# Product 2 of two groups as one block product, rows scaled by halves, loads one at a time

## Chip, cores and metric

One core of a Trainium2 chip. The metric is the device time of one execution in microseconds (us), the median of several runs.

## What is computed

```python
def reference(a, b, gamma, eps):          # a, b: 2048 x 2048 f32, gamma: 2048
    x = np.matmul(a, b)
    rms = np.sqrt(np.mean(x ** 2, axis=-1, keepdims=True) + eps)
    return (gamma * x / rms).astype(np.float32)
```

A matrix product, then each row is divided by its root mean square and multiplied by gamma.

## The kernel before

**Tiling.** `a` is cut into 16 row blocks of 128, `b` stays in SBUF in bf16 (`raw[j][kp]`: half j of N, 1024 columns, and 256 rows of K). Two row blocks, 2g and 2g+1, form a *group* g. Blocks 0 to 3 are the head (plain products, and one group that is partly transformed); groups 2 to 7 are worked by `first_segment`, `segment` and `last_group`, lines 550 to 729, and only these are changed.

**Seven products for eight.** For a group and a half of N, the 256 x 2048 by 2048 x 1024 product is split in two by two by two (rows by block, K into even and odd tiles of 128, columns into chunks of 512), and made with Winograd's seven products: `product(g, j, m, bank)` for m = 1 to 7, each eight matmuls of 128x128 by 128x512 (`KP` = 8) into one PSUM bank. Product 1 is A11 B11 and product 2 is A12 B21. The right-hand sums lie in `sums[j]` and, for one of them, in place in `raw`; the left-hand sums `s_sum` are made for each group by `a_sums(g, which)` on VectorE from the transposed row blocks `at(2g)` and `at(2g+1)`. Sum 2 is the left operand of product 6, sum 3 of product 7, sum 4 of product 3, sum 1 (in place in the odd block) of product 5.

**Half groups and segments.** `halves` lists (g, j); n is the index, so n = 0 is group 2 left, n = 4 group 4 left, n = 10 and 11 group 7. `do(n, m)` issues product m of half group n; `take(n, what)` moves a result out of PSUM into an `x` tile in SBUF. Partial results pass from bank to bank: after product 1, ScalarE copies bank B1 to B2 (line 528); product 6 adds into B2; ScalarE copies B2 to B3 (530); product 5 adds into B3; VectorE's `take 22` makes the bottom right chunk of B3 and of product 7 (which ScalarE copied, 532); product 4 adds into B2 and `take 21` makes the bottom left; product 3 adds into B3, and `take 12` (540) is the top right; product 2 adds into B1, and `take 11` (538) is the top left. So product 3 has to wait for take 22, which reads the bank that it adds to.

`segment(n)` issues, in this order, product 6 of n, product 3 of n-1, product 2 of n, product 1 of n+1, products 7, 5 and 4 of n. Around them it weaves the work on the rows to come and on those that are done. The order of each engine's work is the order of the program (`manual_schedule`): an instruction that waits holds up all behind it on its engine.

**Rows to come.** A row block is loaded to `a32` (two buffers, on POOL's queue). In the left segment of group g, blocks 2g+2 and 2g+3 are readied: `row_norm` (two squares and a root on ScalarE), `prepare` = `row_factor` (four small VectorE operations), `row_apply` (scale to fp16, 2048 wide, line 240), `transpose_dma` (on SP's queue, line 199). In the right segment `a_sums(g + 1, ...)` makes the sums from them. `load_after(src, mb)` has POOL copy one column of `src` (line 140), so that the load of block mb is issued only when `src` is there; in a left segment the load of 2g+4 follows the transposed block 2g+2, in a right one that of 2g+5 follows the transposed block 2g+3.

**Rows that are done.** `square_half` and `square_right` square x on ScalarE (line 267), the latter with the root; `finish` (line 306) multiplies both halves by 1/rms and gamma on VectorE and issues the outputs on SP. Blocks 2g-1 and 2g-2 are finished in the left segment of group g. x tiles are eight slots, shared out by `slot_of` (line 248).

**The end.** `last_group` has its own order for group 7 (lines 630 to 729): product 2 of its right half, then `square_of`, root and inverse for block 14, product 7, then product 4 of the left half and sixteen matmuls of 256 columns for block 15, whose sums are added to the banks on VectorE before (line 699).

Of the kernel before, what the change touches and what calls it, by code (L numbers as in the profile page):

```python
# [17 lines left out]
def kernel(  # L18
# [13 lines left out]
    nc = tc.nc  # L32
# [11 lines left out]
    NG = MB // 2  # L44
    G0 = HB // 2
    PAIR = G0 - 1

    ctx.enter_context(tc.manual_schedule())
    consts = ctx.enter_context(tc.tile_pool(name="consts", bufs=1))
# [32 lines left out]
    def a16_slot(mb):  # L82
        if mb == HB + 1:
            return a16_first
        if mb == HB:
            return x_slot[2 * HB - 1].bitcast(FP16)
        return head_flat.bitcast(FP16)[:, (2 + mb % 2) * K:(3 + mb % 2) * K]

    s_sum = {s: consts.tile([P, KP, P], FP16, name=f"s_{s}") for s in (2, 3, 4)}

    def at(mb):
        return (at_even, at_odd)[(mb // 2) % 2][:, mb % 2]
# [105 lines left out]
    def transpose_dma(mb):  # L198
        nc.sync.dma_start_transpose(at(mb), a16[mb])
# [17 lines left out]
    def row_norm(mb):  # L217
        n2 = stat_pool.tile([P, 2], FP32, name="n2")
        for h in range(2):
            junk = sq_pool.tile([P, 2 * CH], BF16, name="sq")  # L220
            nc.scalar.activation(out=junk, in_=a32[mb][:, h * HALF:(h + 1) * HALF],  # L221
                                 func=ACTF.Square, scale=2.0 ** -8, accum_out=n2[:, h:h + 1])
        norm[mb] = stat_pool.tile([P, 1], FP32, name="norm")
        nc.scalar.activation(out=norm[mb], in_=n2[:, 0:1], func=ACTF.Sqrt, bias=n2[:, 1:2],  # L224
                             scale=1.0)
# [12 lines left out]
    def row_apply(mb):  # L238
        a16[mb] = a16_slot(mb)
        nc.vector.tensor_scalar_mul(out=a16[mb], in0=a32.pop(mb), scalar1=factor.pop(mb))  # L240

    def prepare(mb):
        row_factor(mb)
        row_apply(mb)
        transpose_dma(mb)

    x_half = {}
    slot_of = {(r, h): r + HB * h for r in range(HB) for h in range(2)}

    for n, slots in enumerate(((0, 4, 1, 5), (2, 6, 3, 7), (4, 5, 0, 1), (6, 7, 2, 3),  # L250
                               (5, 1, 4, 0), (7, 3, 6, 2))):
        for m, slot in enumerate(slots):
            slot_of[HB + 2 * n + m % 2, m // 2] = slot

# [15 lines left out]
    def square_half(mb, h):  # L270
        square_of(mb, x_tile(mb, h))
# [73 lines left out]
    def product_matmul(g, j, m, bank, kp, start):  # L345
        lhsT = {1: lambda: quarter(g, 0, 0), 2: lambda: quarter(g, 0, 1),
                3: lambda: sum_of(g, 4), 4: lambda: quarter(g, 1, 1), 5: lambda: sum_of(g, 1),
                6: lambda: sum_of(g, 2), 7: lambda: sum_of(g, 3)}[m]()
        rhs = {1: lambda: b_quarter(j, kp, 0, 0), 2: lambda: b_quarter(j, kp, 1, 0),
               3: lambda: b_quarter(j, kp, 1, 1), 4: lambda: sums[j][:, 2, kp, :],  # L350
               5: lambda: b_quarter(j, kp, 0, 1), 6: lambda: sums[j][:, 0, kp, :],
               7: lambda: sums[j][:, 1, kp, :]}[m]()
        nc.tensor.matmul(bank, lhsT[:, kp, :], rhs, start=(start and kp == 0),  # L353
                         stop=(kp == KP - 1), skip_group_check=not start)

    def product(g, j, m, bank, start=True):
        for kp in range(KP):
            product_matmul(g, j, m, bank, kp, start)

# [157 lines left out]
    def do(n, m, copies=True):  # L519

        if n >= len(halves) or n < 0:
            return
        g, j = halves[n]
        b1, b2, b3 = B1[n % 2], B2[n % 2], B3[n % 2]
        product(g, j, m, {1: b1, 2: b1, 3: b3, 4: b2, 5: b3, 6: b2, 7: B7}[m],
                start=m in (1, 7))
        if m == 1:
            nc.scalar.copy(out=b2, in_=b1)  # L528
        elif m == 6:
            nc.scalar.copy(out=b3, in_=b2)  # L530
        elif m == 7 and copies:
            nc.scalar.copy(out=chunks(n)[2], in_=B7)  # L532

    def take(n, what, engine="A"):

        x11, x12, x21, x22 = chunks(n)
        if what == 11:
            copy_on(engine)(out=x11, in_=B1[n % 2])
        elif what == 12:
            copy_on(engine)(out=x12, in_=B3[n % 2])  # L540
        elif what == 22:
            add(x22, B3[n % 2], x21)
        else:
            add(x21, B2[n % 2], x21)

    def load_after(src, mb):
        wait_for(src)
        load_block(mb)

    def first_segment():  # L550
        n, g, j = 0, G0, 0
        nxt = 2 * g + 2
        do(n, 1)
        do(n, 7, False)
        finish(0, (1,))
        pair_ends()
        do(n, 2)
        row_norm(nxt)
        a_sums(g, (4,))
        finish(0, (0,))  # L560
        do(n, 6)
        do(n + 1, 1)
        prepare(nxt)
        do(n, 5)
        nc.scalar.copy(out=chunks(n)[2], in_=B7)
        take(n, 22)
        row_norm(nxt + 1)
        take(n, 11)
        finish(1)
        do(n, 4)  # L570
        prepare(nxt + 1)
        load_after(at(nxt + 1)[:, KT - 1, 0:1], nxt + 2)
        take(n, 21)
        square_half(2 * g + 1, j)

    def segment(n):
        g, j = halves[n]
        ra, rb, nxt = 2 * g, 2 * g + 1, 2 * g + 2
        more = g + 1 < NG
        do(n, 6)  # L580
        if j == 0:
            finish(ra - 1)
            if more:
                row_norm(nxt)
        elif g == G0:
            square_right(r2)
        do(n - 1, 3)
        take(n - 1, 12)
        if j == 0:
            square_right(ra - 2)  # L590
            if more:
                prepare(nxt)
            a_sums(g, (4,))
            finish(ra - 2)
        else:
            square_half(ra, 0)
            if g == G0:
                square_right(r3)
                finish(r2, (1, 0))
        do(n, 2)  # L600
        take(n, 11)
        do(n + 1, 1)
        if j == 0 and more:
            row_norm(nxt + 1)
        if j == 1 and g + 2 < NG:
            load_after(at(nxt + 1)[:, KT - 1, 0:1], nxt + 3)
        if j == 1 and more:
            a_sums(g + 1, (1, 2))
        do(n, 7)
        if j == 1 and more:  # L610
            a_sums(g + 1, (3,))
        do(n, 5)
        take(n, 22)
        if j == 1:
            take_pre(rb)
            take_pre(ra)
        do(n, 4)
        take(n, 21)
        if j == 0:
            square_half(rb, 0)  # L620
            if more:
                prepare(nxt + 1)
            if g + 2 < NG:
                load_after(at(nxt)[:, KT - 1, 0:1], nxt + 2)
        else:
            square_right(rb)
            if g == G0:
                finish(r3, (1, 0))

    def last_group():  # L630
        n = len(halves) - 2
# [11 lines left out]
        def by_r(x, r):  # L643
            nc.scalar.activation(out=x, in_=x, func=ACTF.Copy, scale=r)  # L644

        b2, b3 = [B2[(n + j) % 2] for j in range(2)], [B3[(n + j) % 2] for j in range(2)]
        do(n, 6)
        finish(rb - 2)
        do(n - 1, 3)
        take(n - 1, 12)  # L650
        square_right(ra - 2)
        a_sums(g, (4,))
        do(n, 2)
        take(n, 11)
        do(n + 1, 1)
        do(n, 5)
        nc.scalar.copy(out=x22[0], in_=b3[0])
        finish(ra - 2)
        do(n + 1, 6)
        do(n, 7)  # L660
        add(x22[0], x21[0], x22[0])
        add(b2[0], b2[0], x21[0])
        square_of(rb, x22[0])
        do(n + 1, 5)
        nc.scalar.copy(out=x22[1], in_=b3[1])
        wide = a_pool.tile([P, K], FP32, name="a32")
# [5 lines left out]
        take(n, 12)  # L672
        square_half(ra, 0)
        add(xa, xa, gam_left, ALU.mult)
        do(n + 1, 3)
        take(n + 1, 12)
        square_of(ra, x12[1])
        add(x12[1], x12[1], gam[3], ALU.mult)
        pre_a = stat_pool.tile([P, 1], FP32, name="pre")
        nc.vector.tensor_scalar(out=pre_a, in0=msq[ra][:, 0:1], scalar1=msq[ra][:, 1:2],  # L680
                                scalar2=msq[ra][:, 2:3], op0=ALU.add, op1=ALU.add)
        do(n + 1, 2)
        take(n + 1, 11)
        square_of(ra, x11[1])
        rms_a = root(msq[ra][:, 3:4], pre_a)
        r_a = inverse(rms_a)
        other = B1[0]
        product(g, 1, 7, other)
        nc.scalar.copy(out=x21[1], in_=other)
        halves2 = [slice(0, CH // 2), slice(CH // 2, CH)]  # L690
# [3 lines left out]
        nc.sync.dma_start(out=rows(ra, 0, CH), in_=left)  # L694
        nc.gpsimd.tensor_scalar_mul(out=mid, in0=mid, scalar1=r_a)  # L695
        nc.sync.dma_start(out=rows(ra, CH, HALF), in_=mid)
        nc.vector.tensor_scalar_mul(out=x12[1], in0=x12[1], scalar1=r_a)
        for bank, col in zip(half, halves2):
            add(bank, b2[1][:, col], x21[1][:, col])
        add(x22[1], x21[1], x22[1])  # L700
        scaled_gamma(x11[1], x11[1], r_a, gam[2])
        nc.sync.dma_start(out=rows(ra, HALF, N), in_=x_tile(ra, 1))
        do(n, 4)
        square_of(rb, b2[0])
# [64 lines left out]
```

## Time and profile before

| | |
|---|---|
| median of 3 runs | 223.53 us (223.38 to 223.86) |
| the profiled execution | 222.88 us |
| its span in the trace | 221.1 us |
| mean granted TensorE clock | 0.996 of full speed |
| segments 0 to 9 on TensorE | from 67.3 to 189.65 us |
| last group on TensorE | 189.65 to 214.0 us |
| scaling of a row block to fp16, line 240 | 1.28 us |
| add of a PSUM chunk to an x tile, line 98 | 0.69 us |
| one row block, load to landing | 4.9 to 10.7 us |
| one row block, transpose to landing | 4.2 to 7.2 us |

The span is the time between the first and the last instruction of the trace; the execution's own time has 1.8 us around it. In the trace, PE is TensorE's matmuls, PEld its weight loads, DVE is VectorE, ACT ScalarE, SP and POOL the two queues that issue DMAs (SPq, POOLq). A row of a timeline has the start, the duration, the engine, the line of the program, the operation with its output and inputs, the count, and in brackets the idle time before it with what ended that. A matmul is shown with 0.38 us for its whole way through the array, while the next one starts 0.216 us after it.

### The profile page before, as it was taken

The page shows a single profiled execution, that of the slowest core. Times are in us where ns is not written, and L with a number is a line of the kernel's source. Part 1 is how long each engine was busy: PE and PEld are TensorE (multiplying, and loading weights), DVE is VectorE, ACT ScalarE, POOL GpSimd, SP SyncE. Part 2 cuts the span into 40 slices and gives each one's busy share as a digit, 9 for nine tenths or more (in the row PEclk, how much of TensorE's full clock was granted, in tenths as well). Part 3 has the DMA queues.
Part 4 walks back from the last instruction along what each step waited for, and adds up shares of the span by engine and source line. Part 5 has one row for each costly group of instructions (what it writes and reads, how often), then busy time and mean ns, then how long its engine had stood idle before and what let it go on. Part 6 is the DMA issues. An engine that isn't in the chain of part 4 may idle for free.

```text
span 221.1 us, 2897 instructions
## 1 busy us (share of the span) xinstructions
PE 208.3 (94%) x1012; PEld 97.4 (44%) x1032; DVE 144.4 (65%) x281; ACT 115.7 (52%) x229; POOL 37.7 (17%) x74
## 2 busy tenths in 40 slices
PE   7699999999999999999998999999999999999970
PEld 3344544444454444444443444444444444444440
DVE  2128779999999984988506981688246953583381
ACT  2110002900698558679624966296627964364781
POOL 8544443443000001200101010201010000000030
PEclk9999999999999999999999999999999999999998
DMA  7999999999957486899884499458965874063044
GB/s 147 174 201 205 203 206 210 211 208 237 414 159 329 193 245 135 252 399 342 279 250 193 190 285 284 174 204 224 278 98 213 187 251 86 1 246 138 0 187 193
DMA packets 36719, 46.59 MB, mean 211 GB/s; under 512 B 22240, under 2 KB 26336, under 8 KB 35424
## 3 DMA queue, kind: packets, MB, share of 16 engines
q0 software_dynamic: 10608, 23.86, 43.9%
q1 hardware_dynamic: 25824, 22.29, 33.1%
q10 hardware_dynamic: 272, 0.26, 0.3%
q8 instruction: 8, 0.13, 0.2%
q14 instruction: 7, 0.06, 0.1%
HBM read 34.60 MB, written 16.78 MB: 232 GB/s over the span
## 4 chain that ended last, share of the span: by engine, by line
PE 65%; issue 11%; DMA 10%; ACT 7%; DVE 3%; POOL 1%; ACTq 0%; POOLq 0%; DVEq 0%
PE acc L353 46%; PE acc L366 15%; ACT sq L221 4%; DMA a<-in_a_dram 4%; DMA at_even<-head_at 3%; DMA early<-in_a_dram 3%; PE tbank L392 2%; PE tbank L176 2%; ACT sq L267 1%; DVE a_first L240 1%; POOL b L112 0%; ACT norm L224 0%; ACT sq L717 0%; POOL pace L140 0%; ACT a L644 0%
## 5 line engine op out<-in xcount | busy, mean ns | idle before, releaser
L267 ACT ACTIVATE sq<-x 128x1024 bf16<-128x1024 f32 (+1 forms) x33 | 33.2, 1005 | 30.5 <-DVE x L98 26.6
L353 PEld LDWEIGHTS <-s 128*128 128x128 f16 (+1 forms) x312 | 30.4, 98 | 38.4 <-DVE s L330 1.5
L366 PE MATMUL acc<-b,head_at 128*128 128x512 bf16 x171 | 42.3, 379 | 1.7 <-DMA b<-in_b_dram 1.6
L353 PE MATMUL acc<-b,head_at 128*128 128x512 bf16 x164 | 40.8, 379 | 0.3
L306 DVE SCALAR_TENSOR_TENSOR x<-x,r,gamma_sb 128x1024 f32<-128x1024 f32 x28 | 34.8, 1282 | 0.5
L353 PE MATMUL acc<-b,at_even 128*128 128x512 bf16 x142 | 33.3, 379 | 0.1
L353 PEld LDWEIGHTS <-head_at 128*128 128x128 f16 (+1 forms) x216 | 21.0, 98 | 24.8
L353 PEld LDWEIGHTS <-at_even 128*128 128x128 f16 x192 | 18.8, 98 | 22.6
L353 PE MATMUL acc<-early,s 128*128 128x512 bf16 x108 | 27.1, 379 | 0.2
L221 ACT ACTIVATE sq<-a 128x1024 bf16<-128x1024 f32 x24 | 25.3, 1056 | 1.6 <-DMA a<-in_a_dram 1.2
L366 PEld LDWEIGHTS <-head_at 128*128 128x128 bf16 x176 | 16.9, 98 | 20.8 <-issue 1.7
L353 PE MATMUL acc<-b,s 128*128 128x512 bf16 x103 | 24.3, 379 | 0.3 <-DVE x L98 0.2
L353 PE MATMUL acc<-t_left,s 128*128 128x512 bf16 x95 | 22.5, 379 | 1.0 <-DVE s L330 1.0
L112 POOL DMA_DIRECT2D b<-in_b_dram x32 | 17.2, 540 | 20.8 <-DMA b<-in_b_dram 14.2
L98 DVE TENSOR_TENSOR x<-acc,x 128x512 f32<-128x512 f32 x23 | 15.9, 690 | 6.0 <-ACT x L532 3.3
L402 ACT COPY x<-acc 128x512 f32<-128x512 f32 x7 | 4.1, 580 | 25.5 <-PE acc L366 25.5
L240 DVE TENSOR_SCALAR head_at<-a,s 128x2048 f16<-128x2048 f32 x10 | 12.8, 1278 | 0.0
L330 DVE TENSOR_TENSOR at_even<-at_even 128x1024 f16<-128x1024 f16 x3 | 2.1, 692 | 14.0 <-DMA at_even<-head_at 14.0
L181 DVE COPY head_at<-tbank 128x1024 bf16<-128x1024 bf16 x7 | 4.8, 692 | 9.2 <-PE tbank L176 9.2
L528 ACT COPY acc<-acc 128x512 f32<-128x512 f32 x12 | 6.9, 578 | 6.7 <-PE acc L353 6.7
L695 POOL TENSOR_SCALAR x<-x,r 128x512 f32<-128x512 f32 x1 | 1.9, 1852 | 46.5 <-DVE r L288 46.5
L288 DVE RECIPROCAL r<-rms 128x1 f32<-128x1 f32 x16 | 2.6, 160 | 10.8 <-ACT rms L283 10.7
(103 smaller groups left out, 207.4 us busy)
## 6 DMA issues: line engine op xcount, KB each, us to landing
out_dram<-x SPq DMA_DIRECT2D x29, 512.0 KB, 3.2
a<-in_a_dram POOLq DMA_DIRECT2D x10, 1024.0 KB, 6.0
b<-in_b_dram POOLq DMA_DIRECT2D x32, 256.0 KB, 10.1
a<-in_a_dram POOLq DMA_DIRECT2D x4, 512.0 KB, 9.8
early<-in_a_dram POOLq DMA_DIRECT2D x7, 256.0 KB, 10.2
gamma_sb<-in_gamma_dram POOLq DMA_DIRECT2D x2, 512.0 KB, 9.9
out_dram<-x SPq DMA_DIRECT2D x3, 256.0 KB, 2.5
out_dram<-a SPq DMA_DIRECT2D x1, 768.0 KB, 3.3
```

What stands on the lines that cost most here:

```text
L98: nc.vector.tensor_tensor(out=out, in0=in0, in1=in1, op=op)
L112: nc.gpsimd.dma_start(out=raw[j][kp][:, t, :], in_=b[lo:lo + P, j * HALF:(j + 1) * HALF])
L176: nc.tensor.matmul(view[:, t, r, :], ah(kp)[:, r, t * P:(t + 1) * P], identity, is_transpose=True, start=(t == 0 and r == 0), stop=(t == 1 ...
L181: nc.vector.tensor_copy(out=head_at[:, 2 * kp:2 * kp + 2, :, :], in_=view)
L221: nc.scalar.activation(out=junk, in_=a32[mb][:, h * HALF:(h + 1) * HALF], func=ACTF.Square, scale=2.0 ** -8, accum_out=n2[:, h:h + 1])
L240: nc.vector.tensor_scalar_mul(out=a16[mb], in0=a32.pop(mb), scalar1=factor.pop(mb))
L267: nc.scalar.activation(out=sq[:, 0:src.shape[-1]], in_=src, func=ACTF.Square, scale=inv_sqrt_n, accum_out=msq[mb][:, c:c + 1])
L306: nc.vector.scalar_tensor_tensor(out=x, in0=x, scalar=inverse_of[mb], in1=gamma_sb[:, h * HALF:(h + 1) * HALF], op0=ALU.mult, op1=ALU.mult)
L353: nc.tensor.matmul(bank, lhsT[:, kp, :], rhs, start=(start and kp == 0), stop=(kp == KP - 1), skip_group_check=not start)
L366: nc.tensor.matmul(bank, head_at[:, kt, r, :], head_rhs(c, kt), start=(kt == 0), stop=(kt == KT - 1))
L392: nc.tensor.matmul(tbank, head_at[:, 2 * kp + t, g[0], :], head_rhs(g[1], 2 * kp + t), start=(t == 0), stop=(t == 1))
L528: nc.scalar.copy(out=b2, in_=b1)
```

## The change

Groups 4 and 5 form a pair, and so do 6 and 7. Product 2 is left out of the halves of these groups. In its place one block product is made for the pair: the A12 of two groups (two row blocks) by the B21 of both halves of N, with K cut in two, is again a two by two by two product, and is made with seven steps of four matmuls (`KQ` = 4) for eight. `step(g, m, bank)` issues a step. Its right-hand sums (`b_two`, 16 adds of 512) are made once, in segments 3 to 5; its left-hand sums (`a_two_sums`, four adds of 512) for each pair, in the right segment of its first group, between that segment's a_sums. The steps are woven into `block_segment`, which takes the place of segment 6, and into `last_group`. The bank of the transposes, `tbank`, and the two B1 banks become X2, W2 and Y2.

From product 1 of group 4 on, product 1 goes straight to bank B2, and ScalarE copies it to the top left x chunk, to which the block's result is added later by VectorE. So the squares and the finish of a pair's first row block come later: `finish(8)` in segment 7, `finish(12)` in the last group after product 7.

From row block 10 on, `prepare` scales a row by halves of 1024 and transposes each half with a DMA of its own; the second half lands in the row's own f32 buffer. The loads of blocks 2g+4 and 2g+5 are now both issued in the right segment of group g, the first after block 2g+3 is transposed, the second after the first has landed.

```diff
+    G2 = G0 + 2
+    KQ = KP // 2
...
+    t_two = {2: a16_first.bitcast(BF16), 3: head_flat[:, 2 * K:3 * K], 4: head_flat[:, 3 * K:4 * K]}
+    t_two = {s: t.rearrange("p (k n) -> p k n", k=KQ) for s, t in t_two.items()}
+    y_two = x_slot[5].bitcast(FP16).rearrange("p (s k m) -> p s k m", s=4, k=KQ)
+    a16_half = consts.tile([P, HALF], FP16, name="a16_half")
...
     def prepare(mb):
         row_factor(mb)
-        row_apply(mb)
-        transpose_dma(mb)
+        if mb < 2 * (G2 + 1):
+            row_apply(mb)
+            transpose_dma(mb)
+            return
+        src, f = a32.pop(mb), factor.pop(mb)
+        for h, dst in enumerate((a16_half, src.bitcast(FP16)[:, 0:HALF])):
+            nc.vector.tensor_scalar_mul(out=dst, in0=src[:, h * HALF:(h + 1) * HALF], scalar1=f)
+            nc.sync.dma_start_transpose(at(mb)[:, h * KP:(h + 1) * KP, :], dst)
...
+    def b_two(s):
+        for k in range(KQ):
+            z11, z12, z21, z22 = (z_two(h, j, k) for h in range(2) for j in range(2))
+            out, x, y = {1: (z12, z12, z11), 2: (t_two[2][:, k, :], z22, z12),
+                         3: (t_two[3][:, k, :], z22, z12),
+                         4: (t_two[4][:, k, :], z21, t_two[2][:, k, :])}[s]
+            add(out, x, y, ALU.subtract)
...
+    def a_two_sums(g):
+        a11, a12, a21, a22 = (a_two(g, r, h) for r in range(2) for h in range(2))
+        y1, y2, y3, y4 = (y_two[:, n] for n in range(4))
+        add(y3, a11, a21, ALU.subtract)
+        add(y1, a21, a22)
+        add(y2, y1, a11, ALU.subtract)
+        add(y4, a12, y2, ALU.subtract)
...
+    def step(g, m, bank):
+        for k in range(KQ):
...
+            nc.tensor.matmul(bank, lhsT[:, k, :], rhs, start=(m in (1, 7) and k == 0),
+                             stop=(k == KQ - 1), skip_group_check=m not in (1, 7))
...
         b1, b2, b3 = B1[n % 2], B2[n % 2], B3[n % 2]
+        if g >= G2:
+            b1 = b2
...
-        if m == 1:
+        if m == 1 and g >= G2:
+            nc.scalar.copy(out=chunks(n)[0], in_=b2)
+        elif m == 1:
             nc.scalar.copy(out=b2, in_=b1)
...
     def first_segment():
...
-        load_after(at(nxt + 1)[:, KT - 1, 0:1], nxt + 2)
...
+    X2, W2, Y2 = tbank, B1[1], B1[0]
...
     def segment(n):
...
-            square_half(ra, 0)
+            if not first:
+                square_half(ra, 0)
...
+            elif g == G2:
+                b_two(4)
+            elif not first and g > G2:
+                finish(ra - 2)
-        do(n, 2)
-        take(n, 11)
+        if g < G2:
+            do(n, 2)
+            take(n, 11)
+        if g == G2 - 1 and j == 1:
+            b_two(3)
+            b_two(1)
         do(n + 1, 1)
...
-        if j == 1 and g + 2 < NG:
-            load_after(at(nxt + 1)[:, KT - 1, 0:1], nxt + 3)
+        elif g + 2 < NG:
+            load_after(at(nxt + 1)[:, KT - 1, 0:1], nxt + 2)
+            load_after(a32[nxt + 2][:, 0:1], nxt + 3)
-        if j == 1 and more:
+        if j == 1:
             a_sums(g + 1, (1, 2))
+            if first:
+                a_two_sums(g)
...
             prepare(nxt + 1)
-            if g + 2 < NG:
-                load_after(at(nxt)[:, KT - 1, 0:1], nxt + 2)
+            if g == G2:
+                b_two(2)
...
+    def block_segment(n):
...
+        do(n, 6)
+        finish(ra - 1)
+        step(g - 1, 1, X2)
+        nc.scalar.copy(out=W2, in_=X2)
+        row_norm(nxt)
+        do(n - 1, 3)
+        step(g - 1, 2, W2)
+        step(g - 1, 6, X2)
+        nc.scalar.copy(out=Y2, in_=X2)
+        take(n - 1, 12)
+        add(x00, W2, x00)
+        square_half(ra - 2, 0)
+        prepare(nxt)
+        do(n + 1, 1)
+        step(g - 1, 5, Y2)
+        step(g - 1, 7, W2)
+        add(x11, Y2, x11)
+        take_pre(ra - 2)
+        row_norm(nxt + 1)
+        a_sums(g, (4,))
+        add(x10, W2, x10)
+        add(x11, W2, x11)
+        do(n, 7)
+        step(g - 1, 4, X2)
+        add(x10, X2, x10)
+        do(n, 5)
+        take(n, 22)
+        step(g - 1, 3, Y2)
+        add(x01, Y2, x01)
+        square_right(ra - 2)
+        prepare(nxt + 1)
+        do(n, 4)
+        take(n, 21)
+        square_half(rb, 0)
...
     def last_group():
...
+        x00, x01 = first_sums(n)[0:2]
         do(n, 6)
         finish(rb - 2)
+        step(g - 1, 1, X2)
+        nc.scalar.copy(out=W2, in_=X2)
         do(n - 1, 3)
+        step(g - 1, 2, W2)
+        step(g - 1, 6, X2)
+        nc.scalar.copy(out=Y2, in_=X2)
         take(n - 1, 12)
...
         do(n, 7)
         add(x22[0], x21[0], x22[0])
         add(b2[0], b2[0], x21[0])
         square_of(rb, x22[0])
+        add(x11[1], x11[1], gam[2], ALU.mult)
+        finish(ra - 2)
         do(n + 1, 5)
...
-        do(n + 1, 2)
-        take(n + 1, 11)
-        square_of(ra, x11[1])
         rms_a = root(msq[ra][:, 3:4], pre_a)
```

The steps 5, 7, 4 and 3 with their adds stand in the last group as in the block segment, between its products 1, 5, 6 and 7.

More of the change, by code (lines that the diff above doesn't have):

```diff
@@ L243, in prepare @@
         row_factor(mb)
-        row_apply(mb)
-        transpose_dma(mb)
+        if mb < 2 * (G2 + 1):
[6 more added lines that the diff above has]
+            nc.sync.dma_start_transpose(at(mb)[:, h * KP:(h + 1) * KP, :], dst)
     x_half = {}
     slot_of = {(r, h): r + HB * h for r in range(HB) for h in range(2)}
-    for n, slots in enumerate(((0, 4, 1, 5), (2, 6, 3, 7), (4, 5, 0, 1), (6, 7, 2, 3),
-                               (5, 1, 4, 0), (7, 3, 6, 2))):
+    for n, slots in enumerate(((0, 4, 1, 5), (2, 6, 3, 7), (0, 4, 1, 6), (7, 3, 2, 4),
+                               (6, 1, 0, 3), (4, 2, 7, 1))):
         for m, slot in enumerate(slots):
@@ L358, in product, with z_two, a_two @@
             product_matmul(g, j, m, bank, kp, start)
+    def z_two(h, j, k):
+        return b_quarter(j, h * KQ + k, 1, 0)
+    def b_two(s):
[5 more added lines that the diff above has]
+            add(out, x, y, ALU.subtract)
+    def a_two(g, r, h):
+        return at(2 * (g + r))[:, 1::2, :][:, h * KQ:(h + 1) * KQ, :]
+    def a_two_sums(g):
[7 more added lines that the diff above has]
+        for k in range(KQ):
+            lhsT = {1: lambda: a_two(g, 0, 0), 2: lambda: a_two(g, 0, 1),
+                    3: lambda: y_two[:, 3], 4: lambda: a_two(g, 1, 1), 5: lambda: y_two[:, 0],
+                    6: lambda: y_two[:, 1], 7: lambda: y_two[:, 2]}[m]()
+            rhs = {1: lambda: z_two(0, 0, k), 2: lambda: z_two(1, 0, k), 3: lambda: z_two(1, 1, k),
+                   4: lambda: t_two[4][:, k, :], 5: lambda: z_two(0, 1, k),
+                   6: lambda: t_two[2][:, k, :], 7: lambda: t_two[3][:, k, :]}[m]()
+            nc.tensor.matmul(bank, lhsT[:, k, :], rhs, start=(m in (1, 7) and k == 0),
+                             stop=(k == KQ - 1), skip_group_check=m not in (1, 7))
     def head_rhs(c, kt):
@@ L571, in first_segment, with first_sums @@
         prepare(nxt + 1)
-        load_after(at(nxt + 1)[:, KT - 1, 0:1], nxt + 2)
         take(n, 21)
         square_half(2 * g + 1, j)
+    X2, W2, Y2 = tbank, B1[1], B1[0]
+    def first_sums(n):
+        return [chunks(m)[0] for m in (n - 2, n - 1, n, n + 1)]
     def segment(n):
@@ L579, in segment @@
         more = g + 1 < NG
+        if g >= G2 and (g - G2) % 2 == 1 and j == 0:
+            block_segment(n)
+            return
+        first = g >= G2 and (g - G2) % 2 == 0
         do(n, 6)
@@ L582, in segment @@
             finish(ra - 1)
-            if more:
-                row_norm(nxt)
+            row_norm(nxt)
         elif g == G0:
@@ L590, in segment @@
             square_right(ra - 2)
-            if more:
-                prepare(nxt)
+            prepare(nxt)
             a_sums(g, (4,))
@@ L599, in segment @@
                 finish(r2, (1, 0))
-        do(n, 2)
-        take(n, 11)
+            elif g == G2:
[8 more added lines that the diff above has]
+            b_two(1)
         do(n + 1, 1)
-        if j == 0 and more:
+        if j == 0:
             row_norm(nxt + 1)
-        if j == 1 and g + 2 < NG:
-            load_after(at(nxt + 1)[:, KT - 1, 0:1], nxt + 3)
-        if j == 1 and more:
+        elif g + 2 < NG:
+            load_after(at(nxt + 1)[:, KT - 1, 0:1], nxt + 2)
+            load_after(a32[nxt + 2][:, 0:1], nxt + 3)
+        if j == 1:
             a_sums(g + 1, (1, 2))
+            if first:
+                a_two_sums(g)
         do(n, 7)
-        if j == 1 and more:
+        if j == 1:
             a_sums(g + 1, (3,))
@@ L615, in segment @@
             take_pre(rb)
-            take_pre(ra)
+            if not first:
+                take_pre(ra)
         do(n, 4)
@@ L620, in segment @@
             square_half(rb, 0)
-            if more:
-                prepare(nxt + 1)
-            if g + 2 < NG:
-                load_after(at(nxt)[:, KT - 1, 0:1], nxt + 2)
+            prepare(nxt + 1)
+            if g == G2:
+                b_two(2)
         else:
@@ L628, in segment @@
                 finish(r3, (1, 0))
+    def block_segment(n):
+        g, j = halves[n]
+        ra, rb, nxt = 2 * g, 2 * g + 1, 2 * g + 2
+        x00, x01, x10, x11 = first_sums(n)
+        do(n, 6)
+        finish(ra - 1)
+        step(g - 1, 1, X2)
+        nc.scalar.copy(out=W2, in_=X2)
+        row_norm(nxt)
+        do(n - 1, 3)
[5 more added lines that the diff above has]
+        square_half(ra - 2, 0)
+        prepare(nxt)
+        do(n + 1, 1)
[15 more added lines that the diff above has]
+        square_right(ra - 2)
+        prepare(nxt + 1)
+        do(n, 4)
+        take(n, 21)
+        square_half(rb, 0)
     def last_group():
@@ L646, in last_group @@
         b2, b3 = [B2[(n + j) % 2] for j in range(2)], [B3[(n + j) % 2] for j in range(2)]
+        x00, x01 = first_sums(n)[0:2]
         do(n, 6)
         finish(rb - 2)
+        step(g - 1, 1, X2)
+        nc.scalar.copy(out=W2, in_=X2)
         do(n - 1, 3)
+        step(g - 1, 2, W2)
+        step(g - 1, 6, X2)
+        nc.scalar.copy(out=Y2, in_=X2)
         take(n - 1, 12)
-        square_right(ra - 2)
+        add(x00, W2, x00)
+        square_half(ra - 2, 0)
+        do(n + 1, 1)
+        step(g - 1, 5, Y2)
+        step(g - 1, 7, W2)
+        add(x11[1], Y2, x11[1])
+        take_pre(ra - 2)
         a_sums(g, (4,))
-        do(n, 2)
-        take(n, 11)
-        do(n + 1, 1)
+        add(x11[0], W2, x11[0])
+        add(x11[1], W2, x11[1])
+        square_of(ra, x11[1])
         do(n, 5)
         nc.scalar.copy(out=x22[0], in_=b3[0])
-        finish(ra - 2)
+        step(g - 1, 4, X2)
+        add(x11[0], X2, x11[0])
         do(n + 1, 6)
+        step(g - 1, 3, Y2)
+        add(x01, Y2, x01)
+        square_right(ra - 2)
         do(n, 7)
@@ L674, in last_group @@
         add(xa, xa, gam_left, ALU.mult)
+        pre_a = stat_pool.tile([P, 1], FP32, name="pre")
+        nc.vector.tensor_scalar(out=pre_a, in0=msq[ra][:, 0:1], scalar1=msq[ra][:, 1:2],
+                                scalar2=msq[ra][:, 2:3], op0=ALU.add, op1=ALU.add)
         do(n + 1, 3)
@@ L677, in last_group @@
         square_of(ra, x12[1])
[L678 to L681, printed above, removed]
-        do(n + 1, 2)
-        take(n + 1, 11)
-        square_of(ra, x11[1])
         rms_a = root(msq[ra][:, 3:4], pre_a)
         r_a = inverse(rms_a)
-        other = B1[0]
+        other = X2
         product(g, 1, 7, other)
@@ L696, in last_group @@
         nc.sync.dma_start(out=rows(ra, CH, HALF), in_=mid)
-        nc.vector.tensor_scalar_mul(out=x12[1], in0=x12[1], scalar1=r_a)
+        nc.vector.tensor_scalar_mul(out=x11[1], in0=x11[1], scalar1=r_a)
         for bank, col in zip(half, halves2):
@@ L700, in last_group @@
         add(x22[1], x21[1], x22[1])
-        scaled_gamma(x11[1], x11[1], r_a, gam[2])
+        scaled_gamma(x12[1], x12[1], r_a, gam[3])
         nc.sync.dma_start(out=rows(ra, HALF, N), in_=x_tile(ra, 1))
```

## The prediction

> **What bounds the kernel now.** I read the busy line first, then the stages by windows, then the stalls of TensorE, then the chain around a group's transposes. Rows of a count from 0; group g is row blocks 2g and 2g+1, and n counts half groups (n = 4 is group 4 with the left half of N). "Segment n" starts with product 6 of n.
>
> ```profile
> span 221.1 us, 2897 instructions
> PE 208.3 (94%) x1012; PEld 97.4 (44%) x1032; DVE 144.4 (65%) x281; ACT 115.7 (52%) x229; POOL 37.7 (17%) x74
> ```
>
> ```profile
> 91.46:103.55 12.09, 12.04 (x57) 5.46 (x57) 11.20 (x20) 9.11 (x18) 0.00 (x0) 1.00 1.02 383
> 103.55:117.12 13.57, 12.35 (x56) 5.37 (x56) 5.08 (x10) 6.20 (x13) 2.18 (x4) 1.00 0.80 233
> 117.12:129.22 12.10, 12.05 (x56) 5.50 (x57) 9.77 (x17) 9.64 (x20) 0.00 (x0) 1.00 0.63 211
> 129.22:141.31 12.09, 12.04 (x57) 5.46 (x57) 5.55 (x11) 5.60 (x11) 1.85 (x4) 1.00 0.74 232
> ```
>
> These are segments 2 to 5 (length; then busy PE, PEld, DVE, ACT, POOL; clock; DMA share; GB/s). A segment is 56 matmuls, 12.09 us, so one matmul is 0.216 us and a product of eight 1.73; granted clock 1.00. TensorE is never idle, except in segment 3, which is 1.48 longer. There the trace of waits names two places:
>
> ```profile
> 105.63 1.89 PE L353 MATMUL acc<-b,s 128*128 128x512 bf16 x8 [0.20 <-DVE x L98]
> 108.33 5.22 SPq L199 DMA_TRANSPOSE at_even<-head_at  x1
> 115.59 0.69 DVE L330 TENSOR_TENSOR at_even<-at_even 128x1024 f16<-128x1024 f16 x1 [7.32 <-DMA at_even<-head_at]
> 117.12 1.90 PE L353 MATMUL acc<-t_left,s 128*128 128x512 bf16 x8 [0.97 <-DVE s L330]
> ```
>
> Product 3 starts 0.35 later than its predecessor's start plus 1.73, product 6 of group 4 1.13 later: the transpose of row block 9 needed 7.2 us while the load of block 10 (issued at 107.49) ran. So the bound is TensorE, with one chain close behind it: row_norm, prepare, transpose, a_sums, product 6. How close is shown for group 5:
>
> ```profile
> 133.46 3.74 SPq L199 DMA_TRANSPOSE head_at<-head_at  x1
> 138.74 0.69 DVE L330 TENSOR_TENSOR head_at<-head_at 128x1024 f16<-128x1024 f16 x1 [5.44 <-DMA head_at<-head_at]
> 141.31 1.89 PE L353 MATMUL acc<-t_left,s 128*128 128x512 bf16 x8
> 141.72 0.69 DVE L98 TENSOR_TENSOR x<-acc,x 128x512 f32<-128x512 f32 x1
> 142.51 1.06 ACT L267 ACTIVATE sq<-x 128x1024 bf16<-128x1024 f32 x1 [3.87 <-DVE x L98]
> 143.89 0.58 ACT L530 COPY acc<-acc 128x512 f32<-128x512 f32 x1
> ```
>
> Block 11 lands 2.67 before segment 6 (at 141.31). VectorE then does three sums, take 22 and take 21, ScalarE the square of block 9, and only after it the copy of product 6 (0.85 after that product's end, with nobody waiting).
>
> **Removed.** 32 product-2 matmuls become 28 for each of the two pairs of groups: 8 x 0.216 = **-1.73**. All lie on the bound. Eight ScalarE copies of take 11 (0.57) go, two bank copies per pair come; ScalarE is not the bound, but in segments 4 and 8 the copies stood in the chain: L532, that the block's takes wait for, comes 0.47 earlier.
>
> **Loads one at a time, segments 1 to 3.** Block 8's load is issued at 88.25 and lands 7.9 later (96.2), block 9's at 89.44 and lands 10.7 later (100.1), 3.9 behind the other: so the first was hardly slowed by the second. Now block 9 is issued only after block 8 has landed: 96.2 + 0.7 (POOL copy and issue) + landing. That is 4.9 (load at 116.26, alone) to 6.5 (154.18, beside a transpose); outputs still move, at over 390 GB/s in these microseconds, so I take 6.3: 103.2. row_norm(9) started at 101.73; it now waits 1.5 (bounds 0.1 to 3.1). ScalarE holds L532 behind it, VectorE take 22, and product 3, already 0.35 late, is 1.5 later. In return the transpose of block 9 has no load beside it: rows without one land after 4.2 to 4.4, those with one after 5.3, 6.5 and 7.2. Prepared at 109.8, it lands at 114.1, its sums are ready at 115.7, and product 6, due at 117.45, waits for nothing. The 16 adds of b_two cost 0.42 each (L98 on 128x512 bf16); eight lie in this hole of VectorE's (5.08 busy of 13.57), until 113.2. Nothing but the loads is queued on POOL behind its new wait; SP has outputs and transposes in the same order as before, a half more at a time. Net: +1.5 - 1.13 = **+0.3** (bounds -1.05 to +1.9).
>
> **Segments 4 and 5 (and 8 and 9).** Without product 2 each is 10.36 long, so segment 6 is due 20.72 after segment 4 started, not 24.18. The chain does not shrink as much. From the start of segment 4: take 21 of segment 3 ends at 0.9; square 0.95; copy 2.37; then L530 to the end of L532, 9.16 in segment 6 of before (143.89 to 153.05), less 0.47: 11.0. Take 22 and 21 1.4, row_factor 0.7, and scaling by halves. A 1024-wide half isn't in the trace: 0.485 for 512 (L697) and 1.278 for 2048 (L240) bound it, 0.75 on the line between. First half ready at 13.9, second 14.6. A half transpose isn't there either. A whole one moves its 0.52 MB in some 3 us:
>
> ```profile
> 182.00:183.00 1.00, 1.00 (x7) 0.43 (x5) 0.00 (x0) 1.00 (x3) 0.00 (x0) 1.00 0.89 174
> 183.00:184.00 1.00, 1.00 (x6) 0.45 (x5) 0.00 (x0) 0.53 (x1) 0.00 (x0) 1.00 1.16 216
> 184.00:185.00 1.00, 1.00 (x6) 0.49 (x5) 0.00 (x0) 0.33 (x1) 0.00 (x0) 1.00 0.73 135
> ```
>
> (segment 9; next to last column DMA share, last GB/s.) The engines are full, so halves gain only the earlier start: landing between 13.9 + 4.35 = 18.25 and, if a half costs as much delay as a whole, 14.6 + 4.35 + 0.4 = 19.3; I take 18.6.
>
> Behind the landing t stand, on VectorE, two sums (1.55), the four new a_two_sums (512 wide fp16: between 0.42 of the 512-wide and 0.69 of the 1024-wide rows; 0.46 with dispatch, 1.85), the third sum, take 22 (done t + 4.7), take 21 (t + 5.5); then on ScalarE the square of the odd block (to 6.93), L530 (7.43) and only then the copy of the block's bank, X2 to W2 (8.0). Step 2 accumulates into W2. On TensorE it is due 1.73 + 0.86 + 1.73 = 4.32 after segment 6's start, 25.04; it starts at t + 8.05 = 26.65. Stall **+1.6** (1.2 to 2.3). In the first pair load 11, issued after load 10 has landed (114.1 + 0.75 + 4.9 + 0.75 = 120.5), arrives at 125.4 to 126.3, and row_norm(11) is due at 125.4 (+0 to 0.9): +0.3, so **+1.9**. If the cover of 2.67 were left, both would be nothing. In the second pair loads 14 and 15 come in time.
>
> [...] The windows above show at most 216 GB/s with the engines full, and I go by them. [...]
>
> **Inside the block segments.** Six adds from PSUM (0.69 each), 13.0 us of VectorE in 16.4 of TensorE, and finish(8) moved to segment 7 (3.75 + 2.7 of 10.36): covered. Block 13's sums are ready some 3 us before segment 8. Nothing.
>
> **Last group.** finish(12) (2 x 1.28) now follows product 7 instead of coming eight products earlier, and it stands on VectorE ahead of the gamma products and pre_a. From the end of product 7 of half 10: L532 0.8 to 1.2, two adds 1.3, gamma 0.7, finish 2.7, gamma 0.7, pre_b 0.15, wide gamma 1.23, pre_a 0.27: 7.9 to 8.3; product 7 of half 11 starts at 5.2. root of block 14 comes 2.8 after it; in before (208.65 and 210.22) it was 1.57. The copy L689 and the bank adds behind it are then 0.95 late for the last 16 matmuls (before they ended 0.15 ahead), and VectorE stays behind up to the last inverse: **+1.1** (0.3 to 1.4).
>
> **Sum.** -1.73 + 0.3 + 1.9 + 1.6 + 1.1 = +3.2. The profiled execution took 222.88 (span 221.1 and 1.8 around it): 226.1. The median, 223.53, is 0.65 above that execution; the forecast for the median is **226.7**. The terms' bounds, not all at one end, give 225.3 to 228.3 for this case alone.
>
> **Rivals.**
> 1. *The chain arrives in time (faster).* One mechanism: transposes without loads beside them land so early that the block's copy X2 to W2 is never late. It needs t below 17.0 (halves in 2.4 after the second scaling) and load 9 by 101.7. For it: 4.3 against 7.2. Against: full DMA engines above. Then -1.73 - 1.48 + 1.1 = -2.1: 221.4.
> 2. *Load 9 is in time, the rest as forecast.* For it: block 8 could land earlier when nothing follows it in the queue. Then -1.48 in place of +0.3, first stall 1.6: -1.73 - 1.48 + 1.6 + 1.6 + 1.1 = +1.1: 224.6.
> 3. *Halves cost as much as wholes and the loads drag.* t = 19.3 and load 11 at its late bound: 0.3 - 1.73 + 3.2 + 2.3 + 1.4 = +5.5: 229.0.
> That fewer matmuls run than written can't fail: the loops issue them.
>
> **How the numbers follow.** Chances: forecast 0.48, first rival 0.14, second 0.22, third 0.16. The range for 8 in 10 goes from 223.9, under the second rival's value, to 228.9. A difference of 0.2% (0.45 us) is what the measurement tells from none. Faster 0.13 (most of the first rival, a little of the second), same 0.08 (the low end of the second), slower 0.79.
>
> **What would show it.** Right: 8 TensorE matmuls fewer; no wait at product 6 of group 4, but a longer one at product 3 before it, with row_norm(9) waiting for its load; TensorE idle 1 to 2 us in each block, at step 2, waiting for a ScalarE copy; the last inverse about 1 us later after the last full product. Wrong: step 2 without idle time, or take 22 of segment 2 as early as before.

## The result, and the profile after

The changed kernel takes 231.89 us (median; 231.23 to 232.77), against 223.47 before: a ratio of 1.038, 95% interval 1.034 to 1.042. Slower was forecast, but by 3.2 us, and 8.4 were measured. Executions of one kernel lie up to 2% apart, the longer ones mostly at a lower mean granted clock (experiment 1: 226.75 us at 0.993, 230.70 at 0.977), and each trace below is of one execution (in experiments 1 and 5 the fastest, 226.75 and 228.30 us); what made the others longer no trace shows.

The busy lines of the page of after:

```profile
span 229.7 us, 2952 instructions
PE 211.4 (92%) x1004; PEld 97.9 (43%) x1024; DVE 161.7 (70%) x323; ACT 113.0 (49%) x225; POOL 37.0 (16%) x74
```

Eight matmuls fewer (1004 records for 1012), yet TensorE is busy 3.1 us longer: some matmuls must have been slower. The timeline of after shows which; start and duration, the idle time before in brackets:

```profile
103.53 1.89 PE L367 MATMUL acc<-early,s 128*128 128x512 bf16 x8
110.42 3.57 PE L367 MATMUL acc<-b,s 128*128 128x512 bf16 x8 [5.00 <-DVE x L106]
113.78 3.08 PE L367 MATMUL acc<-b,head_at 128*128 128x512 bf16 x8
116.70 1.89 PE L367 MATMUL acc<-b,at_even 128*128 128x512 bf16 x8
123.61 1.89 PE L367 MATMUL acc<-t_left,s 128*128 128x512 bf16 x8
149.84 1.02 PE L406 MATMUL acc<-b,at_even 128*128 128x512 bf16 x4 [1.03 <-ACT acc L709]
199.27 1.02 PE L406 MATMUL acc<-b,at_even 128*128 128x512 bf16 x4 [1.44 <-ACT acc L762]
220.57 1.91 PE L839 MATMUL acc<-early,head_at 128*128 128x256 bf16 x16 [0.64 <-DVE acc L106]
```

TensorE stands idle for 5.0 us (from 105.42) before product 3 of half 2. That product and the next take 3.36 and 2.92 (difference of starts) for 1.73. Windows of after tell why; columns are length, busy PE, PEld, DVE, ACT, POOL, the granted clock, DMA share, GB/s:

```profile
108.00:109.00 1.00, 0.00 (x0) 0.00 (x0) 0.00 (x0) 0.97 (x3) 0.00 (x0) 1.00 1.07 438
109.00:110.00 1.00, 0.00 (x0) 0.00 (x0) 0.33 (x1) 0.64 (x2) 0.00 (x0) 0.68 0.96 393
110.00:111.00 1.00, 0.58 (x2) 0.25 (x2) 0.90 (x2) 0.00 (x0) 0.00 (x0) 0.50 0.18 70
115.00:116.00 1.00, 1.00 (x4) 0.37 (x3) 1.00 (x3) 0.79 (x2) 0.00 (x0) 0.50 1.16 213
116.00:117.00 1.00, 1.00 (x6) 0.44 (x5) 0.16 (x1) 0.10 (x1) 0.00 (x0) 0.90 0.90 168
```

The 0.68 and the 0.90 are means over a fall and a return within their microsecond: the granted clock falls to 0.50 at 109.4, 3.9 us into the gap, and comes back at 116.2, after 5.8 us of matmuls. What ended the gap is in the timeline of after:

```profile
97.36 0.53 POOL L139 DMA_DIRECT2D a<-in_a_dram  x1 [0.32 <-DVE x L320]
106.51 1.06 ACT L229 ACTIVATE sq<-a 128x1024 bf16<-128x1024 f32 x1 [4.22 <-DMA a<-in_a_dram]
109.67 1.49 DVE L106 TENSOR_TENSOR x<-acc,x 128x512 f32<-128x512 f32 x2 [5.11 <-ACT x L585]
```

Block 9's load is issued at 97.36, after block 8 has landed, and lands 9.1 later. In that time, by a window of after, the DMA engines were full (share 0.98) and moved 2.9 MB (9.13 us at 317 GB/s), of which the load is 1.0:

```profile
97.36:106.49 9.13, 8.01 (x37) 3.52 (x37) 5.87 (x10) 4.81 (x11) 0.53 (x1) 1.00 0.98 317
```

row_norm(9) waits for it on ScalarE; the copy of product 7 (L585) stands behind row_norm in ScalarE's order, take 22 (L106) behind the copy, and product 3 behind take 22. Added up from the two traces, after less before:

| stage | us |
|---|---|
| product 3 of half 2 later (110.42 for 105.63) | +4.79 |
| 16 matmuls at the slow clock (6.28 for 3.45) | +2.83 |
| wait at product 6 of group 4 gone | -1.13 |
| eight matmuls fewer | -1.73 |
| first block: segment 6 takes 17.59 for 16.40 of matmuls | +1.19 |
| second block: step 2 late 1.60; 0.19 before the product ahead of it; segment 9 longer by 0.15 | +1.94 |
| last group: bank adds late 0.58, end 0.13 | +0.71 |
| sum (spans: 229.7 - 221.1 = 8.6) | +8.6 |

### The profile page after: what moved, and what is told of

It is laid out like the page before. It is cut to its first block, busy times and chain, and to the rows that moved or that the text cites. A ratio compares the mean times of both kernels' runs of the same rounds, so it can differ in the third digit from the quotient of the medians.

```text
span 229.7 us, 2952 instructions
## 1 busy us (share of the span) xinstructions
PE 211.4 (92%) x1004; PEld 97.9 (43%) x1024; DVE 161.7 (70%) x323; ACT 113.0 (49%) x225; POOL 37.0 (16%) x74
## 4 chain that ended last, share of the span: by engine, by line
PE 33%; DVE 12%; DMA 7%; ACT 5%; issue 2%; SPq 1%; ACTq 0%; DVEq 0%
PE acc L367 28%; DVE x L106 5%; DMA a<-in_a_dram 4%; PE acc L406 3%; DVE x L320 3%; DMA head_at<-a 3%; DVE s L344 2%; ACT sq L281 2%; PE tbank L406 2%; ACT sq L229 1%; DVE head_at L344 1%; SPq L259 1%; DVE acc L106 1%; DVE a L106 1%; ACT rms L297 1%
## 5 line engine op out<-in xcount | busy, mean ns | idle before, releaser
L415 PE MATMUL acc<-b,head_at 128*128 128x512 bf16 x171 | 42.6, 380 | 0.2
L367 PE MATMUL acc<-b,head_at 128*128 128x512 bf16 x133 | 34.8, 390 | 0.2
L106 DVE TENSOR_TENSOR x<-acc,x 128x512 f32<-128x512 f32 x33 | 22.6, 689 | 15.7 <-ACT x L585 5.1
L367 PE MATMUL acc<-b,s 128*128 128x512 bf16 x100 | 25.9, 399 | 5.2 <-DVE x L106 5.0
L367 PEld LDWEIGHTS <-head_at 128*128 128x128 f16 (+1 forms) x184 | 18.2, 100 | 22.2 <-issue 2.2
L367 PE MATMUL acc<-b,at_even 128*128 128x512 bf16 x110 | 26.2, 379 | 0.2
L367 PE MATMUL acc<-early,s 128*128 128x512 bf16 x103 | 25.5, 379 | 0.1
L367 PEld LDWEIGHTS <-at_even 128*128 128x128 f16 x160 | 15.7, 98 | 18.9
L451 ACT COPY x<-acc 128x512 f32<-128x512 f32 x7 | 4.1, 580 | 25.9 <-PE acc L415 25.9
L106 DVE TENSOR_TENSOR x<-tbank,x 128x512 f32<-128x512 f32 x9 | 6.2, 692 | 4.8 <-PE tbank L441 3.6
L585 ACT COPY x<-acc 128x512 f32<-128x512 f32 x10 | 5.8, 576 | 4.6 <-PE acc L367 4.6
```

What stands on the lines that cost most here:

```text
L106: nc.vector.tensor_tensor(out=out, in0=in0, in1=in1, op=op)
L415: nc.tensor.matmul(bank, head_at[:, kt, r, :], head_rhs(c, kt), start=(kt == 0), stop=(kt == KT - 1))
```

## The experiments

**1. Load 9 early again** (the changed kernel)

```diff
-            load_after(a32[nxt + 2][:, 0:1], nxt + 3)
+            src = at(nxt + 1)[:, KT - 1, 0:1] if g == G0 else a32[nxt + 2][:, 0:1]
+            load_after(src, nxt + 3)
```

> The changed kernel, but block 9's load no longer waits for block 8 to land: it follows the transposed block 7, as before. Theory: the 5.0 us wait at product 3 of segment 2 and the slow clock after it (16 matmuls in 6.28 us for 3.45) both go; segment 4 starts near 116.0 for 123.6, and the time falls by 7.6, to 224.3. The stalls inside the two blocks (1.0 and 1.4) stay. Rival: the wait is that of a crowded VectorE and ScalarE (new sums, other copies); then product 3 stays late and the time stays above 229.

Measured: 228.42 (226.75 to 230.70), ratio 1.020 (1.014 to 1.026). The gap at 105 goes, as the theory has it, and segment 4 starts at 115.72. But a wait appears that after didn't have. Timeline of this run:

```profile
118.77 0.53 POOL L139 DMA_DIRECT2D a<-in_a_dram  x1 [0.37 <-ACT acc L583]
125.22 1.06 ACT L229 ACTIVATE sq<-a 128x1024 bf16<-128x1024 f32 x1 [1.50 <-DMA a<-in_a_dram]
128.38 1.49 DVE L106 TENSOR_TENSOR x<-acc,x 128x512 f32<-128x512 f32 x2 [1.59 <-ACT x L585]
129.12 1.89 PE L367 MATMUL acc<-b,s 128*128 128x512 bf16 x8 [1.15 <-DVE x L106]
143.59 1.02 PE L406 MATMUL acc<-b,at_even 128*128 128x512 bf16 x4 [1.35 <-ACT acc L710]
175.57 1.06 ACT L229 ACTIVATE sq<-a 128x1024 bf16<-128x1024 f32 x1 [1.55 <-DMA a<-in_a_dram]
179.47 1.89 PE L367 MATMUL acc<-b,s 128*128 128x512 bf16 x8 [1.19 <-DVE x L106]
```

Reading down, it is the same chain as before, one pair of rows later: block 11's load, issued only when block 10 has landed, is late for row_norm; take 22 is late; product 3 of half 4 waits 1.15, and so does product 3 of half 8 for block 15. These two waits are about the 2.4 by which the traced execution misses 224.3. The hole at block 9 had hidden them in after, because it had set TensorE back against the later loads: there block 11's load was issued 0.27 after the start of segment 4 (123.88), here 3.05 after it. The waits of 1.35 and 1.44 at step 2 stay, as expected.

**2. TensorE kept at work** (the changed kernel, 22 matmuls into an unused bank)

```diff
+        if n == 2:
+            for i in range(22):
+                nc.tensor.matmul(tbank, sum_of(g, 2)[:, i % KP, :], sums[0][:, 0, i % KP, :],
+                                 start=True, stop=True)
         do(n - 1, 3)
```

> The changed kernel with 22 more matmuls into an unused bank, issued between product 6 of half 2 and product 3 of half 1, 4.75 us of work in the gap of 5.16; the results are not used. Theory (the idle gap itself makes the clock fall): product 3 starts at about the same 110.4, the granted clock stays at 1.00, products 3 and 2 take 1.73 each, and the time falls by 2.8, to 229.1. Rival (the clock falls for another reason, or the slow matmuls wait for data): no gain, 231.9.

Measured: 232.47 (232.02 to 234.02), ratio 1.042 (1.037 to 1.046). The place in the expectation is one segment off: the gap lies before product 3 of half 2, while the filling stands before product 3 of half 1, ten microseconds ahead of it. It still tells something. TensorE runs through without a gap, the clock stays at 1.00 (from 91.5 to 120.66), product 3 of half 2 starts at 110.31 at full speed, and segment 4 at 120.66 for 123.61. From there to the end 3.8 are lost (109.9 for 106.1), so that the span is 0.9 longer than after's. Most of it goes to waits that after didn't have, of 1.72 and 1.19 at product 3 of halves 4 and 8; their delays add up to 3.2. The first of them:

```profile
130.72 1.06 ACT L229 ACTIVATE sq<-a 128x1024 bf16<-128x1024 f32 x1 [2.08 <-DMA a<-in_a_dram]
134.63 1.89 PE L367 MATMUL acc<-b,s 128*128 128x512 bf16 x8 [1.72 <-DVE x L106]
```

Without idle time the clock did not fall, as the theory has it, but the time did not fall either: what TensorE gains, the next chained loads take.

**3. The wait alone** (the kernel before)

```diff
-            load_after(at(nxt + 1)[:, KT - 1, 0:1], nxt + 3)
+            src = a32[nxt + 2][:, 0:1] if g == G0 else at(nxt + 1)[:, KT - 1, 0:1]
+            load_after(src, nxt + 3)
```

> The kernel before, with this one edit: block 9's load waits until block 8 has landed. Theory: the same gap of about 5 us at product 3 and the same slow clock; the 1.1 us at product 6 of group 4 may go, since block 9 is transposed later, clear of block 10's load: +6.5, 230.0. Rival (block product and copies to blame): at most +1, 224.5.

Measured: 228.55 (226.71 to 229.40), ratio 1.021 (1.015 to 1.028). One changed source of one wait makes the kernel before 5.0 slower, with no block product in it. Its timeline:

```profile
111.28 3.21 PE L353 MATMUL acc<-b,s 128*128 128x512 bf16 x8 [5.71 <-DVE x L98]
114.33 1.89 PE L353 MATMUL acc<-b,head_at 128*128 128x512 bf16 x8
```

Windows of this run, the granted clock third from the end:

```profile
110.00:111.00 1.00, 0.00 (x0) 0.00 (x0) 0.47 (x1) 0.50 (x2) 0.24 (x1) 0.79 0.86 340
113.00:114.00 1.00, 1.00 (x4) 0.38 (x3) 0.91 (x1) 0.69 (x3) 0.00 (x0) 0.50 0.98 401
114.00:115.00 1.00, 1.00 (x6) 0.42 (x5) 0.00 (x0) 0.47 (x1) 0.00 (x0) 1.00 0.68 287
```

The gap is there in full, but the clock is back at 114.0 and only one product is slow (3.05), so the clock costs 1.3 here and not 2.8. By the trace, product 3 is 5.65 late, 0.9 more than in after; with 1.3 for the clock and the 1.13 at product 6 gone, that makes 5.8, the difference of the spans (226.9 and 221.1).

**4. The later loads alone** (the kernel before; blocks 10 to 15 loaded in right segments)

```diff
+            if g > G0:
+                load_after(at(nxt + 1)[:, KT - 1, 0:1], nxt + 2)
-            load_after(at(nxt + 1)[:, KT - 1, 0:1], nxt + 3)
+            src = at(nxt + 1)[:, KT - 1, 0:1] if g == G0 else a32[nxt + 2][:, 0:1]
+            load_after(src, nxt + 3)
...
-            if g + 2 < NG:
-                load_after(at(nxt)[:, KT - 1, 0:1], nxt + 2)
```

> The kernel before, with only the later loads moved: blocks 10 to 15 are loaded in the right segments, one at a time, blocks 8 and 9 as before. Theory: transposes land after 4.3 us for 5.3 to 7.2, the 1.13 at product 6 of group 4 goes and nothing else changes: 222.4. Rival (the second load of each pair is late for row_norm as block 9's was): VectorE's take 22 late, waits at product 3, 224 or more.

Measured: 221.90 (median of ten), ratio 0.993 (0.990 to 0.996). The loads, moved, win 1.6 by the medians, 0.5 more than expected; the spans show 1.2 of it (219.9 for 221.1), the 1.13 and 0.12 of the 0.35 at product 3 of half 2. The theory on the transposes holds for one of each pair only. Those of blocks 9, 11 and 13 land after 4.2 to 4.3 us (before 7.2, 5.3 and 6.5), but those of blocks 10, 12 and 14 now have the second load beside them and take 6.8 to 7.9 (before 4.3 to 4.8); these have time to spare. With segments of 12.09 us the chain is in time, and TensorE has no other wait left.

**5. The pair's sums later** (experiment 1, with one call moved)

```diff
             a_sums(g + 1, (1, 2))
-            if first:
-                a_two_sums(g)
...
             square_right(rb)
+            if first:
+                a_two_sums(g)
```

> The run with block 9's load early, and the pair's four left-hand sums moved behind take 21 and the square of the odd block. Theory: take 21 and the square come 1.85 earlier, so the copy X2 to W2 is in time and the waits of 1.35 and 1.44 at step 2 go; the waits at product 3 of halves 4 and 8 (1.15 and 1.19, behind row_norm of blocks 11 and 15, whose loads are late) stay. 2.8 less than that run: 224.0 against its best of 226.75. Rival (the copy is late because ScalarE is full): the waits at step 2 stay, 226.7 or more.

Measured: 229.12 (228.30 to 230.39), ratio 1.023 (1.017 to 1.029). Half right: both waits at step 2 are gone (take 21 comes 1.4 earlier against product 6), but the time isn't. Timeline of this run:

```profile
177.85 1.06 ACT L229 ACTIVATE sq<-a 128x1024 bf16<-128x1024 f32 x1 [3.26 <-DMA a<-in_a_dram]
181.76 3.21 PE L367 MATMUL acc<-b,s 128*128 128x512 bf16 x8 [4.07 <-DVE x L106]
```

The wait at product 3 of half 8 grows from 1.19 to 4.07, and the slow clock comes with it (the product takes 3.05 for 1.73). TensorE is due there only 0.6 earlier than in experiment 1; the other 2.3 are block 15, which lands at 177.8 for 175.5. Its load is the last of a chain: block 13's load took 8.6 for 5.8 (the outputs beside it come 1.4 earlier), its transpose landed 1.0 later, and loads 14 and 15 follow that transpose.

**6. Loads by two** (experiment 1, with the second load of a pair behind the first, without waiting for it to land)

```diff
-            src = at(nxt + 1)[:, KT - 1, 0:1] if g == G0 else a32[nxt + 2][:, 0:1]
-            load_after(src, nxt + 3)
+            load_block(nxt + 3)
```

> The run with block 9's load early, and each later pair of loads issued together after the odd block's transpose, not one at a time. Theory: blocks 11 and 15 land some 3 us earlier, so the waits at product 3 of halves 4 and 8 go; the copy X2 to W2 stays late by 1.2 to 1.6. 224.4 against the best of 226.75. Rival (product 3 waits for work of VectorE, not for loads): 226.7.

Measured: 223.63 (median of ten), ratio 1.002 (0.998 to 1.006). The waits at product 3 of halves 4 and 8 go; at step 2 two remain:

```profile
142.13 1.02 PE L406 MATMUL acc<-b,at_even 128*128 128x512 bf16 x4 [1.02 <-ACT acc L709]
191.10 1.02 PE L406 MATMUL acc<-b,at_even 128*128 128x512 bf16 x4 [1.34 <-ACT acc L762]
212.40 1.91 PE L839 MATMUL acc<-early,head_at 128*128 128x256 bf16 x16 [0.42 <-DVE acc L106]
```

Changing the loads alone takes the changed kernel from 231.89 back to the time before.

**7. All three** (5 and 6 together, and in the last group one gamma product forward)

```diff
         add(x11[0], X2, x11[0])
+        add(x11[1], x11[1], gam[2], ALU.mult)
...
-        add(x11[1], x11[1], gam[2], ALU.mult)
         finish(ra - 2)
```

> Both edits together, and in the last group the gamma product of block 14's third chunk moved forward into VectorE's idle time before product 7. Theory: no wait at product 3, none at step 2, the last 16 matmuls 0.4 to 0.6 earlier: 226.75 - 2.3 - 2.8 - 0.5 = 221.1. Rival (the waits are passed on to the next place): 223 or more.

Measured: **220.19** (219.86 to 220.59), ratio 0.982 (0.978 to 0.987): faster than both kernels. TensorE has no wait of note left from half 2 to the end. Timeline of this run, at the places where the others waited:

```profile
112.93 1.05 POOL L139 DMA_DIRECT2D a<-in_a_dram  x2
123.73 1.06 ACT L229 ACTIVATE sq<-a 128x1024 bf16<-128x1024 f32 x1
127.93 1.89 PE L367 MATMUL acc<-b,s 128*128 128x512 bf16 x8
140.88 1.03 PE L406 MATMUL acc<-b,at_even 128*128 128x512 bf16 x4
209.34 1.91 PE L839 MATMUL acc<-early,head_at 128*128 128x256 bf16 x16
```

The two loads are issued 0.5 apart and land after 5.1 and 7.0, that is the second at 120.5; one at a time (experiment 1) it landed at 125.2. No bracket stands behind row_norm(11), product 3, step 2 or the last 16 matmuls.

**8. The control** (experiment 4 with loads by two as in 6: no block product, no halves)

> The kernel before with the loads of blocks 10 to 15 in the right segments, each pair issued together. The control for the one above: the loads' gain without the block product. Theory: as with one at a time, 221.7, since no row_norm waited there. Rival (one at a time was late there too): 220.5 or less.

Measured: 221.67 (221.37 to 224.84), ratio 0.988 (0.983 to 0.994). As with one at a time: in the longer segments of before the second load was in time either way. Against this control the rest of the change, repaired and with the gamma edit, is worth 1.5 by the medians (220.19 for 221.67), of the 1.73 of its eight matmuls; three of the control's four executions lie at 221.37 to 221.79, which gives 1.2 to 1.6.

## Why the prediction was wrong

- **Loads one at a time, segments 1 to 3: here it failed.** The mechanism was the one forecast, down to the order (load 9, row_norm, L532, take 22, product 3), and the 1.13 at product 6 did go. The size was wrong twice. The landing, taken as 6.3 and bounded by 4.9 and 6.5, was 9.1, after an issue 0.5 later than taken: the bounds were a load alone and one beside a transpose, and this one moved beside four outputs and the transpose of block 8, which itself took 6.9. So the wait was 4.8 and not 1.5, past its bound of 3.1. The rows of before held the warning: block 8's load, hardly slowed by the second as the prediction says, took 7.9 beside outputs (8.4 in after, with no other load), and its transpose 5.9 with no load beside it, where the prediction has 4.2 to 4.4 for such rows. And the idle time had a second price that no term held, the slow clock: 2.83. Together, with the -1.13, +6.5 stood where +0.3 was forecast. Experiment 1 takes the wait on load 9 out of the changed kernel and both prices go; experiment 3 puts it into the kernel before and both come.
- **When the second price comes.** The granted clock fell 3.9 us (after) and 5.0 (experiment 3) into gaps of 5.0 and 5.7, and came back after 5.8 and 2.7 us of matmuls; from fall to return it was slow for 6.8 and 3.4 us, the one twice the other. Behind the gap of 4.1 in experiment 5 the product took the same 3.05 as in experiment 3. Behind the last matmul of all the clock fell after 2.9 us in after (from 222.5 to 225.4) and after 5.3 in before (from 214.0 to 219.4). Behind waits of up to 1.7 no product was slow (1.72 behind the wait of 1.72 in experiment 2, for 1.73). So the forecast's own wait of 1.5 lay among those that had no such price, and only its bound of 3.1 lay above the shortest idle time with a fall: the second price came with the size of the first.
- **Eight matmuls**: -1.73, as forecast.
- **Chain behind the transpose.** Block 11's sums began 18.58 after segment 4's start, for a landing taken as 18.6. The block's copy was late as described; step 2 was late by 1.19 and 1.60, for 1.6 each, and 0.34 came just before the second. (The cover of 2.67 in before is 2.6: block 11 landed at 138.72.) Experiment 5 showed the cause, the four sums ahead of take 21. But the late loads of this step were priced for the first pair alone and at 0.3. In after they cost nothing, by luck of the first hole; experiments 1 and 2 showed waits of 1.15 to 1.72 for both pairs, once that hole no longer hides them.
- **Halves of a transpose.** From the first scaling to the sums, a whole row takes 5.71 (block 11 in the control) and halves 5.43 (in the fastest version): they gain 0.3. The prediction's landing at 18.6 is 5.5 after its first scaling (at 13.1), so the size was about right.
- **Last group**: +0.71 for +1.1. The mechanism holds: root of block 14 comes 2.64 after the start of product 7 of half 11 (forecast 2.8, before 1.57), and TensorE waits 0.64 for the bank adds. VectorE's chain from the end of product 7 of half 10 to pre_a took 7.6, for 7.9 to 8.3 in the sum.
- **Rivals.** The third, halves as dear as wholes and dragging loads, had the right culprit in its second half, but at 0.9 and at block 11, not at 9. The first and second needed load 9 in time, which it was not.

No run shows the gamma edit by itself, the late load 9 in the fastest version, or halves in the kernel before, so what each of these is worth alone stays open.

## What to carry to other kernels

When a wait is put on a load so that it runs alone, price the whole latency of issue and landing that now stands in series, beside everything else that moves then, and ask of each faster stage whether the chained loads can keep its pace. Two loads issued 0.5 us apart in one queue landed one after the other (after 5.1 and 7.0 us, experiment 7); issuing the second early costs the first nothing that these runs show (block 10 lands after 5.1 us either way). And an idle gap of TensorE of four microseconds or more cost more than itself in these runs: 1.3 or 2.8 us on top, for the clock. Waits of up to 1.7 had no such price (1.72 for the product behind the longest); no gap between 1.7 and 4.1 was seen.

## What the runs showed of the hardware

The price of an idle gap was not the same in each run: 16 matmuls in 6.28 us after 5.0 us of idle time (after), 8 in 3.05 after 5.7 (experiment 3) and 8 in 3.05 after 4.1 (experiment 5), for 3.45 and 1.73 at full clock. The longest gap did not cost most. The slow clock lasted 6.8 us in after and 3.4 in experiment 3, and the matmuls began 1.1 and 0.7 us after its start; why it lasted twice as long in after no run shows.

Loads, transposes and outputs took longer beside each other. In before a transpose took 4.3 alone, 5.3 to 7.2 beside a load and 5.9 beside outputs (block 8); a load took 4.9 alone (block 11), and in after 8.4 beside outputs (block 8) and 9.1 beside outputs and a transpose (block 9). How much of the 9.1 is the transpose's, these rows don't tell.
